# Loads, idle products and an order: the entry, the first pairs and the last down part of a two-FFN encoder block

## The chip, the cores and the metric

One core of one Trainium2 chip runs the whole block in one launch. The metric is the device time of that launch in microseconds, as the median of several runs. A profiled execution has a time of its own, and its span runs from the first instruction to the last.

## The reference

The kernel computes one layer on 512 tokens of width 1024, with 16 learned meta tokens set in front (528 columns in all), in float32:

```python
h = concat(meta, x)
f = swiglu(rmsnorm(h, g1), w_gate1, w_up1, w_down1)      # 1024 -> 2816 -> 1024
h = h + 0.5 * rmsnorm(f, post1)
h = h + rmsnorm(mixer(rmsnorm(h, mix_pre)), mix_post)    # two attentions, gated
f = swiglu(rmsnorm(h, g2), w_gate2, w_up2, w_down2)
h = h + 0.5 * rmsnorm(f, post2)
return h[16:]
```

with `swiglu(h) = (silu(h @ w_gate) * (h @ w_up)) @ w_down`. The two feed-forward blocks and their borders are what the change touches; the mixer between them stays as it is.

## The kernel before, in words

**Precision.** A float32 operand is split into a rounded high part (a cast on ScalarE, line 190) and a remainder (a subtraction on VectorE, line 195). Each product is three TensorE products of such parts, hi.hi, hi.lo and lo.hi (`mm3`, lines 165 to 169). Weights arrive as float32 through SyncE's DMA queue (line 157) and are split on arrival, so every weight tile costs a load, a cast and a subtraction.

**Order.** The program text is put in order by a scheduler that simulates the engines; instructions written inside `high_priority` go ahead of others that are ready, and `after(x)` puts an instruction behind `x` on `x`'s engine. On each engine, and in SyncE's queue, the order is then fixed and the engine works strictly in it.

**Buffers.** PSUM has eight tiles of 128 x 512, by tags: `z` (4), `b` (2), `y` (2). Scratch tiles of 128 x 528 are `T` (7 buffers, lines 108 and 64). Summed inputs and other split tiles share tag `u` (8 buffers).

**Entry** (`entry`, lines 292 to 333). The 528 columns go in two halves of 272 and 256. For the first half, eight input tiles are loaded, squared on ScalarE, and each square is summed over its partitions by one-column float32 products on TensorE (line 309). Mean, power -0.5 (on GpSimd, line 244) and a spread over the partitions (line 251) give the factor by which VectorE scales the inputs (line 325) before they are split. The loads of the second half (line 332) are issued after the first weight halves; its squares stand behind the splits of the first half, and its sums and chain come after them.

**Feed-forward block** (`ffn`, line 540). There are 22 tiles of 128 hidden units, in three phases of 6, 8 and 8; after each phase `down` adds the phase's share of the output. The tiles 0 and 1 (`first_two`, line 557) are multiplied half by half, four PSUM outputs side by side (`products`, line 572). Tiles 2 and 3 are `plain` (line 600). The other 18 go as nine pairs (`pair`, line 468): a two-by-two block product with seven products for gate and seven for up instead of eight, each of four k steps, in the order of `PAIR_ORDER` (line 30). Of these, `11`, `12` and `d` take the inputs as they are; `a`, `b`, `c` and `22` take sums of input tiles that `moving` (line 446) makes once per block, after the plain tiles: for each of four j, four half-width operations and two splits, with results named `mab` and `mcd`. On the weight side each pair needs the sums `ws` (lines 498 and 500).

**Down of the first block** (`down_cols`, line 639). In the last phase five column tiles are computed and handed to `post` one half at a time (lines 668 to 675); `post` (line 336) adds the earlier share from PSUM (line 344), squares, scales, multiplies with h, squares again, and adds three of these to running sums (line 357). The remaining three column tiles follow by halves in `emit`.

Of the kernel before, what the change touches and what calls it, by code (L numbers as in the profile page):

```python
# [9 lines left out]
F32 = mybir.dt.float32  # L10
F32R = mybir.dt.float32r
AF = mybir.ActivationFunctionType
# [5 lines left out]
P = 128  # L18
# [10 lines left out]
PHASES = ((0, 6), (6, 8), (14, 8))  # L29
PAIR_ORDER = "g11 g12 ga gb gc u11 u12 gd g22 ua ub uc u22 ud"  # L30
# [36 lines left out]
CHAIN_PRIO = 300  # L67
MLA_SCALE = float((64 + 32) ** -0.5)
# [13 lines left out]
class Block:  # L82
# [115 lines left out]
    def consts(self, cvec, ident, tri, ms):  # L198
        nc = self.nc

        def load(name, src, w):
            t = self.cp.tile([P, w], F32, name=name)
            (nc.scalar if name == "cv" else nc.sync).dma_start(t, src)
            return t
        self.cv = load("cv", cvec, V_END)
        pre = nc.scalar.preload_act_table_set("silu_and_others")
# [8 lines left out]
        def late(mixer):  # L215
            if not mixer:
                self.ident = load("ident", ident, P)
                return
# [73 lines left out]
    def entry(self, xT):  # L292
        nc = self.nc
        self.h = [self.S(f"h{k}") for k in range(KT)]
        self.hh = []
        for hf, half in enumerate(H528):
            w, ns = half.w, len(half.slices)
            sl = slice(half.c0, half.c0 + w)
            pn = self.y("nsum")
            nc.vector.memset(pn[:, 288:288 + ns], 0.0)  # L300
            for k in range(KT):
                if hf == 0:
                    nc.sync.dma_start(self.h[k][:, sl], xT[k, :, sl])
                q = self.T("sq")
                with self.after(self.first[k][0] if hf else None):
                    nc.scalar.activation(q[:, :w], self.h[k][:, sl], AF.Square)
                for s, (c, n) in enumerate(half.slices):
                    c -= half.c0
                    nc.tensor.matmul(pn[:n, 288 + s:289 + s], q[:, c:c + n], self.ones[:, 0:1], start=False,
                                     stop=k == KT - 1, skip_group_check=True)  # L310
            if hf == 0:
                self.late(False)
                yield
            with self.tc.high_priority(ENTRY_PRIO):
# [5 lines left out]
                self.spread(pn, r, half)  # L320
# [8 lines left out]
            if hf == 0:  # L329
                c = slice(w, L)  # L330
                for k in range(KT):
                    nc.sync.dma_start(self.h[k][:, c], xT[k, :, c])
# [113 lines left out]
    def moving(self, W):  # L446
# [4 lines left out]
        self.mv = {n: [] for n in ("11", "12", "a", "b", "c", "22", "d")}  # L451
# [1062 lines left out]
```

## Time and profile before

| | |
|---|---|
| median of 3 runs | 1246.59 us (1243.51 to 1247.79) |
| the profiled execution | 1245.64 us, span 1243.8 us |
| TensorE busy | 1196.5 us, 96% of the span |
| VectorE, ScalarE, GpSimd busy | 828.2, 636.3, 114.8 us |
| mean granted TensorE clock | 0.982 |
| chain that ended last | TensorE 77%, VectorE 10%, DMA 5%, ScalarE 3% |

A row of a timeline gives start, duration, engine, line of the code, operation, written tile, read tiles and shapes; xN says that N instructions were merged into it, and the brackets give the idle time of that engine just before it with what ended it. In a row of windows each engine has its busy time and, in parentheses, the number of its instructions; after the engines stand the granted TensorE clock (PEclk, 1.00 is full), the busy share of the DMA engines and their GB/s. PE is TensorE, PEld its weight loads, DVE VectorE, ACT ScalarE, POOL GpSimd, SP SyncE; SPq is SyncE's queue. Matmuls are pipelined, so neighbouring rows overlap.

### The profile page before, as it was taken

To read this page: it belongs to the slowest core of one execution; us is meant where nothing else is said; L and a number is where in the kernel's file an instruction comes from. 1 tells how busy PE (TensorE), PEld (TensorE's weight loads), DVE (VectorE), ACT (ScalarE), POOL (GpSimd) and SP (SyncE) were. 2 spreads that over 40 slices of the span, in tenths; PEclk is the share of its full clock that TensorE was granted. 3 is DMA by queue.
4 is the path that set the end of the run, shared out by engine and by line. 5 is a ranking of instruction groups with operands and counts; after the bars stand their busy time and mean duration, and the time that the engine had idled before them with its cause. 6 is when DMAs were issued, how large, how long until landed. Compare 5 with 4: busy or idle time off the path is not lost.

```text
span 1243.8 us, 20731 instructions
## 1 busy us (share of the span) xinstructions
PE 1196.5 (96%) x7950; PEld 1080.0 (87%) x7950; DVE 828.2 (67%) x1631; ACT 636.3 (51%) x1368; POOL 114.8 (9%) x189
## 2 busy tenths in 40 slices
PE   7999999999998999999999999999998999999997
PEld 7999999999998887878876777768887899889987
DVE  4493687468857854646666767489766588458855
ACT  4353465235545454656667657566354456325542
POOL 0000000000000001110010243270000000000004
PEclk9889999999998999999999999999899999999999
DMA  7123234322432341222223134353143224413351
GB/s 228 52 61 93 86 103 124 115 67 87 155 110 84 112 139 43 78 85 85 99 97 93 64 114 154 107 194 119 35 153 119 76 95 125 122 59 103 119 170 68
DMA packets 46594, 130.29 MB, mean 105 GB/s; under 512 B 5368, under 2 KB 8824, under 8 KB 46496
## 3 DMA queue, kind: packets, MB, share of 16 engines
q1 hardware_dynamic: 46352, 128.95, 32.3%
q8 instruction: 62, 1.02, 0.3%
q14 instruction: 36, 0.29, 0.1%
q10 hardware_dynamic: 144, 0.04, 0.0%
HBM read 114.99 MB, written 12.58 MB: 103 GB/s over the span
## 4 chain that ended last, share of the span: by engine, by line
PE 77%; DVE 10%; DMA 5%; ACT 3%; issue 3%; POOL 1%; SPq 1%; DVEq 0%; ACTq 0%; POOLq 0%
PE pu L167 4%; PE pu L169 4%; PE pg L167 4%; PE pu L168 4%; PE pg L168 3%; PE pg L169 3%; PE down L719 3%; PE down L718 3%; PE down L717 3%; DVE wp L195 2%; PE start L168 2%; PE start L169 2%; PE start L167 2%; PE gt L167 2%; PE gt L169 2%
## 5 line engine op out<-in xcount | busy, mean ns | idle before, releaser
L190 ACT CAST wp<-ws 128x512 fp32r<-128x512 f32 x144 | 87.3, 621 | 84.5 <-DVE ws L500 55.3
L195 DVE TENSOR_TENSOR wp<-ws,wp 128x512 fp32r<-128x512 f32 x144 | 96.8, 686 | 23.0 <-ACT wp L190 22.6
L195 DVE TENSOR_TENSOR wdl<-wdr,wdh 128x1024 fp32r<-128x1024 f32 (+1 forms) x42 | 49.1, 1170 | 48.6 <-ACT wdh L190 24.2
L190 ACT CAST wdh<-wdr 128x1024 fp32r<-128x1024 f32 (+1 forms) x42 | 42.4, 1009 | 58.1 <-PE pu L169 21.7
L167 PE MATMUL down<-g,wdh 128*128 128x272 f32 (+1 forms) x208 | 60.8, 296 | 4.1 <-DVE f L344 3.7
L167 PE MATMUL pu<-un,wp 128*128 128x264 f32 (+1 forms) x216 | 61.2, 284 | 0.0
L168 PE MATMUL pu<-un,wp 128*128 128x264 f32 (+1 forms) x216 | 60.7, 281 | 0.0
L168 PE MATMUL pg<-un,wp 128*128 128x264 f32 (+1 forms) x216 | 60.6, 282 | 0.0
L168 PE MATMUL down<-g,wdh 128*128 128x272 f32 (+1 forms) x208 | 60.6, 294 | 0.0
L169 PE MATMUL pu<-un,wp 128*128 128x264 f32 (+1 forms) x216 | 60.4, 282 | 0.1
L167 PE MATMUL pg<-un,wp 128*128 128x264 f32 (+1 forms) x216 | 60.5, 282 | 0.0
L169 PE MATMUL pg<-un,wp 128*128 128x264 f32 (+1 forms) x216 | 60.3, 282 | 0.0
L169 PE MATMUL down<-g,wdl 128*128 128x272 f32 (+1 forms) x208 | 60.2, 293 | 0.0
L718 PE MATMUL down<-wdl,g 128*128 128x512 f32 x144 | 56.8, 394 | 0.0
L719 PE MATMUL down<-wdh,g 128*128 128x512 f32 x144 | 56.0, 394 | 0.0
L717 PE MATMUL down<-wdh,g 128*128 128x512 f32 x144 | 54.0, 394 | 0.0
L190 ACT CAST wp<-wpr 128x512 fp32r<-128x512 f32 x54 | 32.1, 621 | 33.4 <-DMA wpr<-g2p 16.5
L167 PE MATMUL pg<-mcd,wp 128*128 128x264 f32 (+1 forms) x144 | 42.3, 294 | 3.1 <-ACT kept L490 3.0
L167 PEld LDWEIGHTS down<-g,wdh 128*128 128x128 f32 x208 | 40.8, 197 | 4.7 <-ACT p L362 3.9
L498 DVE TENSOR_TENSOR ws<-wpr 128x1024 f32<-128x1024 f32 x18 | 22.1, 1225 | 33.1 <-DMA wpr<-g1p 16.5
L169 PE MATMUL pu<-mab,wp 128*128 128x264 f32 (+1 forms) x144 | 41.1, 286 | 2.4 <-DVE wp L195 2.4
L168 PE MATMUL pg<-mab,wp 128*128 128x264 f32 (+1 forms) x144 | 41.2, 287 | 1.5 <-DVE mab L195 1.4
(465 smaller groups left out, 4363.1 us busy)
## 6 DMA issues: line engine op xcount, KB each, us to landing
wdr<-d SPq DMA_DIRECT2D x38, 512.0 KB, 3.5
wpx<-u1p SPq DMA_DIRECT2D x18, 512.0 KB
wpr<-g1p SPq DMA_DIRECT2D x18, 512.0 KB, 3.7
wpx<-u2p SPq DMA_DIRECT2D x18, 512.0 KB, 4.7
wpr<-g2p SPq DMA_DIRECT2D x18, 512.0 KB, 3.7
wgtr<-w_in SPq DMA_DIRECT2D x16, 512.0 KB, 3.6
wxr<-w_out SPq DMA_DIRECT2D x8, 512.0 KB, 3.7
gl<-gates SPq DMA_DIRECT2D x16, 256.0 KB, 4.5
```

The source lines that it names most:

```text
L167: mm(out, wh, xh, start=first, stop=False, skip_group_check=True)
L168: mm(out, wh, xl, start=False, stop=False, skip_group_check=True)
L169: return mm(out, wl, xh, start=False, stop=last, skip_group_check=True).ins
L190: self.cast = nc.scalar.copy(hi, src).ins
L195: return nc.vector.tensor_tensor(lo, src, hi.bitcast(F32), ALU.subtract).ins
L498: TT(*sums[m], ALU.add)
L717: mm(o, gt[:, 0, s], wh, start=fi == 0, stop=False, skip_group_check=True)
L718: mm(o, gt[:, 0, s], wl, start=False, stop=False, skip_group_check=True)
L719: mm(o, gt[:, 1, s], wh, start=False, stop=fi == nf - 1, skip_group_check=True)
```

## The change

It has five parts. In `entry`, both halves of all eight inputs are loaded ahead of the weights, squared, and the squares are added on VectorE into one tile `accx`, so that the partition sums need one product per slice of tokens; 16 products of a tile of ones with itself go on TensorE at the start, four behind the first half's sums and four behind its spread (`turn_over`, `WARM`). The identity matrix is loaded through ScalarE's queue. In `products`, two of the four PSUM outputs of a second half come from tag `b`, and the gate weights of tile 2 are asked for right after the second half's chain. `moving` runs in two parts, one ahead of each plain tile. The first pair of each block takes `FIRST_ORDER`, where `u11` and `u12` come third and fourth. And in the last phase of the first block's down, each column tile's two PSUM halves are added to one full-width scratch tile, on which `post` runs once.

```diff
@@ -27,6 +27,7 @@
 PHASES = ((0, 6), (6, 8), (14, 8))
+FIRST_ORDER = "g11 g12 u11 u12 ga gb gc gd g22 ua ub uc u22 ud"
 PAIR_ORDER = "g11 g12 ga gb gc u11 u12 gd g22 ua ub uc u22 ud"
@@ -65,6 +66,7 @@
 CHAIN_PRIO = 300
+WARM = 16, 4, 4
 MLA_SCALE = float((64 + 32) ** -0.5)
@@ -200,9 +202,10 @@
             t = self.cp.tile([P, w], F32, name=name)
-            (nc.scalar if name == "cv" else nc.sync).dma_start(t, src)
+            (nc.sync if name == "ms" else nc.scalar).dma_start(t, src)
             return t
         self.cv = load("cv", cvec, V_END)
+        self.ident = load("ident", ident, P)
         pre = nc.scalar.preload_act_table_set("silu_and_others")
@@ -212,10 +215,7 @@
 
-        def late(mixer):
-            if not mixer:
-                self.ident = load("ident", ident, P)
-                return
+        def late():
             trif = self.T("trif")
@@ -293,31 +293,41 @@
         self.hh = []
+        acc = self.tp.tile([P, 528], F32, name="accx", tag="acc", bufs=3)
+        idle = self.b("idle")
+
+        def turn_over(n, behind=None):
+
+            with self.after(behind):
+                for _ in range(n):
+                    nc.tensor.matmul(idle[:, :P], self.ones, self.ones, start=True, stop=True)
+        turn_over(WARM[0])
+        for half in H528:
+            sl = slice(half.c0, half.c0 + half.w)
+            for k in range(KT):
+                nc.sync.dma_start(self.h[k][:, sl], xT[k, :, sl])
+                q = acc if k == 0 else self.T("sq")
+                nc.scalar.activation(q[:, sl], self.h[k][:, sl], AF.Square)
+                if k:
+                    nc.vector.tensor_tensor(acc[:, sl], acc[:, sl], q[:, sl], ALU.add)
+        yield
         for hf, half in enumerate(H528):
             w, ns = half.w, len(half.slices)
             sl = slice(half.c0, half.c0 + w)
-            pn = self.y("nsum")
-            nc.vector.memset(pn[:, 288:288 + ns], 0.0)
-            for k in range(KT):
+            with self.tc.high_priority(ENTRY_PRIO):
+                pn = self.y("nsum")
+                nc.vector.memset(pn[:, 288:288 + ns], 1.0)
+                x = self.sums(pn, 288, acc, half)
                 if hf == 0:
-                    nc.sync.dma_start(self.h[k][:, sl], xT[k, :, sl])
-                q = self.T("sq")
-                with self.after(self.first[k][0] if hf else None):
-                    nc.scalar.activation(q[:, :w], self.h[k][:, sl], AF.Square)
-                for s, (c, n) in enumerate(half.slices):
-                    c -= half.c0
-                    nc.tensor.matmul(pn[:n, 288 + s:289 + s], q[:, c:c + n], self.ones[:, 0:1], start=False,
-                                     stop=k == KT - 1, skip_group_check=True)
-            if hf == 0:
-                self.late(False)
-                yield
-            with self.tc.high_priority(ENTRY_PRIO):
+                    turn_over(WARM[1], x)
                 hh = self.cp.tile([P, 4], F32, name=f"hh{hf}")
                 self.mean(hh[:, :ns], pn[:, 288:288 + ns], ns, 1.0 / D)
...
                 r = self.tiny("r")
                 self.rsqrt(r[:, :ns], hh[:, :ns], ns)
-                self.spread(pn, r, half)
+                x = self.spread(pn, r, half)
+                if hf == 0:
+                    turn_over(WARM[2], x)
                 done = []
@@ -326,10 +336,6 @@
             self.first = done
-            if hf == 0:
-                c = slice(w, L)
-                for k in range(KT):
-                    nc.sync.dma_start(self.h[k][:, c], xT[k, :, c])
             yield half
@@ -443,13 +449,14 @@
 
-    def moving(self, W):
+    def moving(self, W, tiles):
 
         nc = self.nc
         H = W // 2
         STT = nc.vector.scalar_tensor_tensor
-        self.mv = {n: [] for n in ("11", "12", "a", "b", "c", "22", "d")}
-        for j in range(4):
+        if tiles[0] == 0:
+            self.mv = {n: [] for n in ("11", "12", "a", "b", "c", "22", "d")}
+        for j in tiles:
             t1, t2 = self.tn[j], self.tn[j + 4]
@@ -465,7 +472,7 @@
 
-    def pair(self, srcs, W, ga, gb):
+    def pair(self, srcs, W, ga, gb, order):
 
@@ -506,7 +513,7 @@
         out = {"11": Y, "b": Y, "c": Y, "22": Y, "12": X, "a": Z, "d": Z}
-        for step in PAIR_ORDER.split():
+        for step in order.split():
             m, n = "gu".index(step[0]), step[1:]
@@ -570,7 +577,7 @@
             def products(half):
-                zz = [self.z("start") for _ in range(4)]
+                zz = [(self.b if half.c0 and o < 2 else self.z)("start") for o in range(4)]
                 c = slice(half.c0, half.c0 + half.w)
@@ -590,6 +597,8 @@
             h1 = next(start)
+            with self.after(self.first[-1][0] if fresh else self.ready):
+                self.ahead = self.wload(gate[2], 1024, "wg")
             acts(h0, zz)
@@ -601,8 +610,11 @@
             for src, n in ((gate[f], "wg"), (up[f], "wu")):
-                with self.hold(f == 2 and not fresh):
-                    wh, wl = self.wload(src, 1024, n)
+                if f == 2 and n == "wg":
+                    wh, wl = self.ahead
+                else:
+                    with self.hold(f == 2 and not fresh):
+                        wh, wl = self.wload(src, 1024, n)
                 o = self.two("gu")
@@ -622,17 +634,17 @@
                 elif f < NPL:
+                    x = f - 2
+                    self.moving(W, (2 * x, 2 * x + 1))
                     plain(f)
                     if f == TURN_AT and not fresh:
                         self.turn()
                     f += 1
-                    if f == NPL:
-                        self.moving(W)
                 else:
                     new_g(f)
                     new_g(f + 1)
                     x = (f - NPL) // 2
-                    self.pair([p[x] for p in pairs], W, g[f], g[f + 1])
+                    self.pair([p[x] for p in pairs], W, g[f], g[f + 1], PAIR_ORDER if x else FIRST_ORDER)
                     f += 2
@@ -665,6 +677,7 @@
                         acc(o, w, half, fi, f0, n)
+                f = self.T("f") if final else None
                 for half, o in outs:
@@ -672,7 +685,9 @@
                     else:
-                        self.post(m, half, o, *tail)
+                        nc.vector.tensor_tensor(f[:, half.c0:half.c0 + half.w], o, fg, ALU.add)
+                if final:
+                    self.post(m, Half(0, L, None), f, tail[0], False, tail[2])
         kept = {}
@@ -828,7 +843,7 @@
 
-        self.late(True)
+        self.late()
         next(start)
         ws = [self.wload(a["w_in"][W_G + j], 1024, "wgt", self.spare(j) if j < 2 else None) for j in range(4)]
         for hf in range(2):
```

## Rows read from the trace of the kernel before

**Rows 1.** The page, part 1: TensorE's busy time, share and instructions.

```profile
PE 1196.5 (96%) x7950; PEld 1080.0 (87%) x7950; DVE 828.2 (67%) x1631; ACT 636.3 (51%) x1368; POOL 114.8 (9%) x189
```

**Rows 2.** Timeline of TensorE in the entry.

```profile
3.58 8.73 PE L309 MATMUL nsum<-ones,sq 128*16 128x1 f32 x48 [3.58 <-ACT sq L306]
...
16.96 1.27 PE L167 MATMUL start<-un,wfh 128*128 128x272 f32 x4 [1.04 <-ACT un L190]
...
31.93 2.51 PE L309 MATMUL nsum<-ones,sq 128*128 128x1 f32 x22
35.47 1.22 PE L251 MATMUL nsum<-ident,r 128*128 128x128 f32 x4 [1.03 <-POOL r L244]
37.70 1.22 PE L167 MATMUL start<-un,wfh 128*128 128x256 f32 x4 [1.01 <-ACT un L190]
...
50.79 0.28 PE L167 MATMUL gu<-un,wgh 128*128 128x272 f32 x1
```

**Rows 3.** Windows: start:end, length, busy time of each engine, PEclk, DMA, GB/s.

```profile
3.00:9.00 6.00, 5.42 (x31) 5.27 (x31) 0.17 (x1) 3.18 (x8) 0.00 (x0) 1.00 0.88 239
16.90:20.50 3.60, 3.54 (x16) 3.54 (x17) 3.56 (x9) 3.60 (x11) 0.00 (x0) 1.00 0.43 118
37.70:41.20 3.50, 3.50 (x16) 3.50 (x17) 3.50 (x10) 1.96 (x5) 0.00 (x0) 0.50 0.02 5
85.40:92.40 7.00, 6.76 (x29) 6.14 (x30) 5.68 (x11) 4.50 (x9) 0.00 (x0) 0.52 0.41 136
93.00:100.00 7.00, 7.00 (x59) 7.00 (x59) 1.30 (x2) 2.55 (x5) 0.00 (x0) 1.00 0.38 103
389.40:392.70 3.30, 3.30 (x17) 3.30 (x17) 2.85 (x8) 1.58 (x4) 0.00 (x0) 0.51 0.01 2
933.00:942.00 9.00, 5.14 (x38) 4.32 (x36) 8.35 (x17) 4.65 (x10) 0.00 (x0) 1.00 0.23 65
```

**Rows 4.** Timeline of TensorE in the first block's first pair.

```profile
83.38 0.39 PE L169 MATMUL pu<-mab,wp 128*128 128x264 f32 x1 [0.90 <-DVE wp L195]
...
85.34 0.55 PE L167 MATMUL pg<-mab,wp 128*128 128x264 f32 x2 [0.83 <-ACT mab L190]
```

**Rows 5.** Timelines of VectorE and TensorE at the last down part's end.

```profile
388.29 1.09 DVE L357 TENSOR_TENSOR acc<-acc,p 128x256 f32<-128x256 f32 x3
...
388.52 0.36 PE L167 MATMUL down<-g,wdh 128*128 128x272 f32 x1 [3.70 <-DVE f L344]
```

**Rows 6.** Timeline of ScalarE in the entry.

```profile
3.10 0.83 ACT L306 ACTIVATE sq<-h 128x272 f32<-128x272 f32 x2 [0.66 <-DMA h<-xT]
...
6.59 1.23 ACT L306 ACTIVATE sq<-h 128x272 f32<-128x272 f32 x3 [0.71 <-DMA h<-xT]
...
9.62 2.68 ACT L190 CAST wfh<-wfr 128x512 fp32r<-128x512 f32 x4 [1.80 <-DMA wfr<-g]
```

**Rows 7.** Timeline of VectorE in the entry.

```profile
12.95 0.15 DVE L241 TENSOR_SCALAR hh<-nsum 128x3 f32<-128x3 f32 x1
...
25.06 1.00 DVE L195 TENSOR_TENSOR un<-h,un 128x272 fp32r<-128x272 f32 x2
```

**Rows 8.** Timeline of SyncE's queue: the first half's inputs.

```profile
0.72 3.71 SPq L303 DMA_DIRECT2D h<-xT  x8
```

**Rows 9.** The instructions on tile mx: ns min/median/max, first and last start, forms.

```profile
L195 DVE TENSOR_TENSOR mab<-mx,mab x8: 679/690/698, 74.7 to 937.6; 128x528 fp32r<-128x528 f32 x4, 128x512 fp32r<-128x512 f32 x4
...
L456 DVE TENSOR_TENSOR mx<-h x4: 420/424/425, 69.8 to 81.6; 128x264 f32<-128x264 f32 x4
```

**Rows 10.** Timeline of VectorE around the plain tiles of both blocks.

```profile
50.38 0.42 DVE L551 TENSOR_TENSOR silu<-start,silu 128x256 f32<-128x256 f32 x1 [7.35 <-ACT silu L550]
...
903.58 0.43 DVE L551 TENSOR_TENSOR silu<-start,silu 128x256 f32<-128x256 f32 x1 [5.80 <-ACT silu L550]
...
912.78 1.23 DVE L498 TENSOR_TENSOR ws<-wpr 128x1024 f32<-128x1024 f32 x1 [4.60 <-DMA wpr<-g2p]
```

**Rows 11.** Timeline of TensorE at the second block's second half.

```profile
886.49 0.73 PE L167 MATMUL start<-un,wfh 128*128 128x256 f32 x4 [0.90 <-ACT un L285]
```

## The prediction

> **What bounds the kernel now.** I read the page's busy shares first: TensorE is busy for 1196.5 of 1243.8 us [rows 1], so the time is TensorE's work plus the 47 us in which it stands still plus what the lower clock costs. Only those two can give anything back, since the change removes no product of the two feed-forward blocks. Then I read TensorE's timeline where the change acts, and windows of the same stretches.
>
> The entry comes first. From 3.58 to 12.31 us TensorE does one-column sums, the first product runs at 16.96, the last product of the first half ends about 31.9, the sums of the second half follow, and the second half's first product waits until 37.70. The gate products of tile 2, the third gate tile, begin at 50.79 [rows 2]. Two products of 3 parts, 8 k and 4 outputs are 96 matmuls, and at full clock one takes 7.00/59 = 0.119 us, so a half is 11.4 us. Here the halves take 15.0 and 13.1: in 3.6 and 3.5 us at their starts only 16 matmuls run, where 30 fit [rows 3]. That is the lower of the two levels, 1.2 GHz; the granted clock shows it as 0.50 in the second stretch and not in the first (1.00), so there I go by the counts.
>
> The second place is the first pair of the first block. TensorE waits 0.90 us for a weight remainder and 0.83 us for a cast of a summed input tile [rows 4], then runs 7.0 us at the lower level, 29 matmuls where 59 fit [rows 3]. The third is the same pair in the second block: in 933 to 942 TensorE is busy 5.14 of 9.00 us and VectorE 8.35 [rows 3]. The fourth is the end of the first block's last down part, a wait of 3.70 us for a PSUM evacuation on VectorE [rows 5], with 3.3 us at the lower level behind it [rows 3].
>
> **The change, part by part.**
>
> *Entry, first half.* Removed: 48 sum records of the first half, which keep TensorE until 12.31, 4.5 us after the last square ended at 7.82 [rows 2, 6]. Added: seven adds on VectorE (two ops of 272 columns took 1.00 us [rows 7]; in 3 to 9 us VectorE is busy 0.17 of 6.00 [rows 3]), of which one lies behind the last square, and six sum records at 8.73/48 = 0.18 us. The sums can end at 7.82 + 0.5 + 1.1 = 9.4, the mean runs then and not at 12.95 [rows 7], and by this the first product could start at 16.96 - 3.6 = 13.4. But 8 inputs of 128 KB go on SP's queue ahead of the four first weight halves. SP issues 8 in 3.71 us [rows 8], 16 in some 8, which the transfers cover: at 239 GB/s [rows 3] 1.05 MB more takes 4.4 us. So the first cast of a weight half moves from 9.62 to about 14.0, and four casts in a row take 2.68 us [rows 6], the last remainder a good 0.7 more: all four outputs are fed from 17.4. The second weight halves stand behind the same bytes as before and do not move. By 17.4 about 12 of the 96 matmuls are done; 84 x 0.119 = 10.0, and the sums and spread of the second half, now eight records in between, cost 1.0: the half ends at 28.4. VectorE must by then have given all eight input remainders. Before, it did this half's work in 15.96 to 26.06 [rows 7]; now four weight remainders more (4 x 0.69) and one of 1024 columns fewer (1.2) make 11.7 us from about 13.4, so 25.1. That is enough for TensorE's last k at 27, with 2 us to spare; with that cover gone the half ends as late as VectorE.
>
> *Entry, second half.* Squares, sums and scaling are done under the first half's products, so the wait from 31.9 to 37.7 goes. What is late next is PSUM: two of the four outputs are now in other buffers and start at once, the other two wait for silu and product of the first half, some 0.4 us beyond six matmuls. Then 11.4 us: end at 28.4 + 0.4 + 11.4 = 40.2, against 50.79. **Gain 10.5.** Bounds: the first product stays at 16.96 and the half keeps its 15.0, then 31.9 + 0.4 + 11.4 = 43.7, gain 7.0; or it starts at 13.4 and nothing holds it, then 37.6, gain 13.1. I stand between, because the weights' 14.0 is a transfer rate and not a choice of the order.
>
> *Idle products.* Sixteen of 128 columns are 32 records; the nearest row has four records in 1.22 us at the lower level [rows 2], so 16 take between 4.9 us (full) and 9.8 us, from 1.0 us on. At worst they hold the sums from 8.3 to 10.8, which the weights' 14.0 covers. The eight behind them are 16 records of 0.15 to 0.31 us in TensorE's own waits, except the last four, ahead of the first product, whose cover is the same. Their worth is the clock: up to 1.7 us (16 matmuls in 3.6 us instead of 1.9). Row against rule: before the first product TensorE had 8.73 us without a gap, and still 16.9 to 20.5 ran at the lower level [rows 2, 3]. The Trainium skill (TensorE: Matmul & The Clock Gate, What's actually happening) says that the default state is throttled and that recent busy-ness releases it. Taken as the profile's busy time, that would have the clock up before the first product already, and the idle products would be worth nothing, a sum of 19.0; this trace disagrees for one-column sums.
>
> *Queues.* The identity goes from SP to ScalarE's queue: one issue of some 0.4 us ahead of the table load, hidden by the 0.66 us that ScalarE waits for the first input [rows 6]. The squares of the second half (8 x 0.42) come ahead of the weight casts on ScalarE, where it waited for the weights and now waits longer. The mask table stays on SP. Zero each.
>
> *Summed inputs early (both blocks).* Four tiles, each four half ops of 0.42 and two remainders of 0.69 on VectorE [rows 9]: 3.07 x 4 = 12.3 us, which before fell into the first pair and now stand ahead of the two plain tiles, 6.15 each. What hides them: VectorE idles 7.35 us before the second half's silu in the first block, 5.80 and 4.60 us around the plain tiles of the second [rows 10]. With that cover gone each would delay a plain tile's weights by up to 6.15. In the first block the stalls are worth 0.90 + 0.83 + (59 - 29) x 0.119 = 5.3; the up factors that need no summed tile now come third and fourth and give VectorE 24 matmuls (2.9 us) more. I take **4.5** of it, bounds 0 and 5.3. In the second block 9.00 - 5.14 = 3.9; I take **3.4**, bounds 0 and 3.9. Next late is the weight remainder of each product, one in 1.46 us of TensorE.
>
> *Second block, second half's first products* in other PSUM buffers: they wait 0.90 us for an input cast, not for PSUM [rows 11]. Zero; bounds -1.6 (transposes and up tile that filled in there lose these buffers) and +0.9.
>
> *Last down part at full width.* Per column tile eight ops of half width become four: three halves take 1.09 us, so 8 x 0.36 = 2.9 [rows 5], against 4 x 0.66 = 2.6 (0.69 a lone one). Five tiles: 1.5 us of VectorE ahead of the late evacuation; if that takes as much off the 3.70 and half of the clock's 1.3 (17 matmuls where 28 fit [rows 3]), **2.3**. Bounds: +5.0 if wait and clock both go, -0.3 if an evacuation finds a full op ahead of it instead of a half one.
>
> **Sum**: 10.5 + 4.5 + 3.4 + 2.3 = 20.7, on the profiled execution's 1245.64: 1224.9. That run lies 0.95 under the median of 1246.59; I say **1225**.
>
> **Rivals.**
> - *Weights first.* ScalarE and VectorE cannot give weight halves and inputs together and the first half ends at 31.9 as before; only the gap goes. Entry 7.0, the rest as above: 1228.4. For: VectorE is full there. Against: 2 us to spare.
> - *Lower level again.* TensorE is nearly still between the idle products and the weights (8 to 14 us), the clock falls back, and the first stretch is as slow as before: 1.7 less, 1226.6. For: after the gap at 32 to 37 the granted clock was 0.50 [rows 3].
> - *No relief in the pairs.* The first wait there is for a weight remainder [rows 4]; if VectorE is as late without the summed tiles, 7.9 are missing: 1232.8. Against: 12.3 us less of its work in that stretch.
> - *Slower: summed tiles in front of plain weights.* VectorE works in order, and a 6.15 us block ahead of the remainder that TensorE needs next shows in full. Four blocks are 24.6, and the lower level behind each costs 1.6: 31.0 against a gain of 20.7, so 1255.9. It decides once two thirds of the blocks show on TensorE. Against: rows 10 hold idle time for nearly all.
> - *Nothing happens*: the order on the engines stays as it was, 1245.6.
>
> **How the numbers follow.** Chances: forecast 0.50, weights first 0.17, lower level 0.13, no relief 0.12, slower 0.05, nothing 0.03. About 0.3% (3.7 us) is what a measurement of this kernel can tell from no change. All cases but the last two are faster by more: 0.92 less 0.04 for smaller terms missing together, so faster 0.88, same 0.06, slower 0.06. The forecast's own range is 1219 to 1231. The low end 1216 has the entry at 13.1 and the stalls gone whole with the clock's part; the high end 1238 takes in no relief together with the entry at its bound, and leaves out the last two cases and the tails.
>
> **What would show it.** Right: the third gate tile's first product near 40 us with no gap between the halves; no TensorE wait over 0.5 us in the first pair of either block; granted clock 1.00 through the first pair; the wait at the last down part under 2.5 us. Wrong: a first product later than 17, TensorE waits for remainders in the plain tiles (a new place), or the 12.3 us of summed tiles still beside the pair's products. If the third gate tile comes after 44, the entry's sum is wrong.

## The result, and the profile after

The changed kernel takes 1214.55 us (median of 4 runs, 1213.73 to 1217.79); the kernel before, run beside it, 1245.05 (1241.04 to 1247.79). The ratio is 0.9762, 95% interval 0.9728 to 0.9797: faster by 30.5 us. The forecast was 1225 and a gain of 20.7, and the low end of its range, 1216, lies above the median. The profiled execution took 1213.73 us, its span is 1211.6, 32.2 less than before.

The page's part 1, TensorE, beside [rows 1]: 17.0 us less busy and 15.2 less idle.

```profile
PE 1179.5 (97%) x7928; PEld 1067.2 (88%) x7928; DVE 833.1 (69%) x1628; ACT 634.8 (52%) x1353; POOL 114.4 (9%) x189
```

The timeline of TensorE in the entry, beside [rows 2].

```profile
1.13 6.28 PE L303 MATMUL idle<-ones 128*128 128x128 f32 x32 [1.13 <-DVE ones L214]
8.75 0.74 PE L234 MATMUL nsum<-ones,accx 128*16 128x1 f32 x6 [1.34 <-DVE accx L312]
...
14.35 0.39 PE L169 MATMUL start<-un,wfh 128*128 128x272 f32 x1 [0.46 <-ACT un L192]
14.58 0.51 PE L234 MATMUL nsum<-ones,accx 128*128 128x1 f32 x4
...
26.33 0.28 PE L170 MATMUL start<-un,wfh 128*128 128x256 f32 x1
...
39.96 0.28 PE L169 MATMUL gu<-un,wgh 128*128 128x272 f32 x1
```

Six records of sums stand where 48 stood, and the second half's sums run between the first half's first and second product. The halves now overlap: two products of 256 columns run at 22.3 us (merged into a row that begins with 272), the others from 26.33, while those of 272 go on until 30.4. The third gate tile begins at 39.96, where the kernel before has 50.79.

Windows of the changed kernel: the first products; the first pair of block 1; that of block 2, as far behind the end of its block's plain tiles as the last of [rows 3]; the end of block 1's last down part.

```profile
14.30:17.90 3.60, 3.55 (x25) 3.28 (x26) 3.60 (x9) 3.60 (x9) 0.83 (x1) 1.00 0.82 303
72.40:79.40 7.00, 7.00 (x60) 7.00 (x59) 3.24 (x5) 3.27 (x7) 0.00 (x0) 1.00 0.63 206
907.30:916.30 9.00, 8.97 (x71) 8.38 (x71) 7.50 (x12) 5.81 (x11) 0.00 (x0) 1.00 0.59 193
376.00:382.00 6.00, 5.27 (x31) 5.04 (x30) 4.93 (x18) 2.66 (x5) 1.94 (x9) 0.72 0.26 87
```

Where [rows 3] have 29 matmuls in 7 us of the first pair, there are 60, and in block 2's 9 us 71 where there were 38. TensorE has no wait in the first pair of either block, and none for an evacuation in the last down part. At 376 to 382 the lower level still shows, 0.72 on average.

To see where 32 us went, the span is cut at TensorE's own marks into eight stretches. Each row of the table is one profiled execution. **A**: start to the first pair. **B**: from there to the end of block 1's first down part. **C**: to the start of its last one. **D**: the last down part. **E**: the mixer, to block 2's first product. **F**: to the end of its plain tiles, 2 and 3 (two expectations call this point the end of tile 2). **G**: from there to the end of its first down part; in block 2 the first pair begins before the last plain products end. **H**: the rest. The kernels e1 to e11 are those of the experiments; the profiled execution of e5 ran disturbed throughout (2277.55 us) and is left out, and the same kernel was profiled again as e11.

| kernel | A | B | C | D | E | F | G | H |
|---|---|---|---|---|---|---|---|---|
| before | 74.0 | 61.5 | 205.1 | 68.3 | 459.0 | 59.4 | 57.0 | 259.5 |
| after | 63.2 | 55.7 | 203.9 | 62.0 | 461.6 | 55.3 | 52.3 | 257.6 |
| e1, PSUM tag undone | 63.1 | 55.7 | 203.9 | 63.2 | 457.1 | 56.5 | 51.2 | 258.2 |
| e2, down part by halves | 63.5 | 55.7 | 203.9 | 67.9 | 456.0 | 59.0 | 51.0 | 257.9 |
| e3, no idle products | 64.6 | 55.7 | 203.9 | 63.0 | 458.7 | 59.8 | 50.6 | 258.9 |
| e4, summed tiles late | 63.4 | 59.2 | 203.9 | 63.0 | 458.3 | 56.5 | 57.2 | 258.4 |
| e6, before + full width | 75.4 | 60.5 | 203.9 | 62.0 | 461.8 | 57.0 | 57.0 | 257.9 |
| e7, before + PSUM tag | 74.3 | 61.7 | 204.1 | 69.1 | 459.4 | 56.6 | 56.7 | 258.4 |
| e8, spread late | 62.9 | 55.7 | 203.9 | 63.4 | 460.1 | 59.0 | 52.1 | 258.0 |
| e9, idle at the borders | 63.3 | 55.7 | 203.9 | 64.8 | 459.7 | 58.1 | 51.0 | 257.9 |
| e10, weights first | 65.1 | 55.7 | 203.9 | 62.0 | 458.2 | 54.1 | 52.2 | 257.9 |
| e11, old pair order | 63.2 | 55.7 | 203.9 | 62.0 | 462.1 | 56.8 | 51.7 | 258.8 |

Before to after: A 10.8, B 5.8, C 1.2, D 6.3, E -2.6, F 4.1, G 4.7, H 1.9. The forecast had 10.5, 4.5, 0, 2.3, 0, 0, 3.4, 0. D and F hold 8.1 of the 11.5 that it missed.

### The profile page after: what moved, and what is told of

It reads as the page before. It is cut to its first block, busy times and chain, and to the rows that moved or that the text cites. A ratio compares the mean times of both kernels' runs of the same rounds, so it can differ in the third digit from the quotient of the medians.

```text
span 1211.6 us, 20678 instructions
## 1 busy us (share of the span) xinstructions
PE 1179.5 (97%) x7928; PEld 1067.2 (88%) x7928; DVE 833.1 (69%) x1628; ACT 634.8 (52%) x1353; POOL 114.4 (9%) x189
## 4 chain that ended last, share of the span: by engine, by line
PE 86%; DVE 6%; ACT 3%; issue 2%; DMA 2%; POOL 1%; SPq 0%; DVEq 0%; ACTq 0%; POOLq 0%
PE pg L169 5%; PE pu L171 5%; PE pg L171 5%; PE pu L170 5%; PE pu L169 5%; PE pg L170 5%; PE down L732 3%; PE down L734 3%; PE down L733 3%; PE down L169 2%; PE down L171 2%; PE down L170 2%; PE gt L169 2%; PE gt L171 2%; PE gt L170 2%
## 5 line engine op out<-in xcount | busy, mean ns | idle before, releaser
L169 PE MATMUL pg<-un,wp 128*128 128x264 f32 (+1 forms) x216 | 60.5, 282 | 0.0
L169 PE MATMUL down<-g,wdh 128*128 128x272 f32 (+1 forms) x208 | 59.4, 290 | 0.4 <-ACT wdh L192 0.4
L170 PE MATMUL down<-g,wdh 128*128 128x272 f32 (+1 forms) x208 | 59.0, 287 | 0.0
L733 PE MATMUL down<-wdl,g 128*128 128x512 f32 x144 | 56.8, 394 | 0.0
L169 PE MATMUL pg<-mcd,wp 128*128 128x264 f32 (+1 forms) x144 | 41.0, 285 | 1.7 <-ACT kept L497 1.7
L171 PE MATMUL pu<-mab,wp 128*128 128x264 f32 (+1 forms) x144 | 40.9, 284 | 0.0
L171 PE MATMUL pg<-mcd,wp 128*128 128x264 f32 (+1 forms) x144 | 40.9, 284 | 0.0
L170 PE MATMUL pg<-mcd,wp 128*128 128x264 f32 (+1 forms) x144 | 40.8, 283 | 0.0
L170 PE MATMUL pu<-mab,wp 128*128 128x264 f32 (+1 forms) x144 | 40.8, 283 | 0.0
```

What stands on the lines that cost most here:

```text
L169: mm(out, wh, xh, start=first, stop=False, skip_group_check=True)
L170: mm(out, wh, xl, start=False, stop=False, skip_group_check=True)
L171: return mm(out, wl, xh, start=False, stop=last, skip_group_check=True).ins
L733: mm(o, gt[:, 0, s], wl, start=False, stop=False, skip_group_check=True)
```

## The experiments

**e1. The second half's first products back in one kind of PSUM buffer.**

```
-  zz = [(self.b if half.c0 and o < 2 else self.z)("start") for o in range(4)]
+  zz = [self.z("start") for o in range(4)]
```

> The changed kernel with all four PSUM outputs of a second half in tag z again. Theory A (the 4.1 us that the second block's start gained, forecast as 0, came from the PSUM tag: with free outputs the spread of the second half runs in the middle of the first half's products and no gap stands ahead of the second half): about 4 us slower there (span +4), with a TensorE gap of 1 us or more and the lower clock back at the second block's second half, and 0 to 1 us in the first block. Theory B (it came from the early gate weights of tile 2 or from the order around it): within 1 us of the changed kernel, no gap.

Measured: 1213.94 us (1211.00 to 1217.85), ratio 0.9749 (0.9721 to 0.9778). F 56.5, G 51.2, A 63.1: F and G together lose 0.1 us, A nothing, and TensorE has no wait between block 2's halves, so the buffers are not what pays in F. The prediction's zero for them holds, and the theory made after the result fell.

**e2. The last down part evacuated by halves again** (`post` for each half, as before).

> The changed kernel with the last down part evacuated by halves again. Theory A (full width alone bought the 6.3 us between the last pair's end and the mixer's first product): about 6 us slower there, with a TensorE wait of some 3.7 us for an evacuation and the lower clock behind it; and if the 2.6 us that the mixer lost also come from the order that full width leaves behind, the mixer is 2 to 3 us shorter, so 3 to 6 us slower in all. Theory B (the gain is from earlier weights or clock, not from full width): under 2 us there.

Measured: 1217.64 us (1216.63 to 1219.96), ratio 0.9783 (0.9760 to 0.9806). D is 67.9, nearly as in the kernel before (68.3), and TensorE waits 3.1 us for an evacuation. The whole loses less than D because E came out at 456.0.

**e6. The other way round: the kernel before with full width alone.**

```
+  f = self.T("f") if final else None
   for half, o in outs:
...
-      self.post(m, half, o, *tail)
+      nc.vector.tensor_tensor(f[:, half.c0:half.c0 + half.w], o, fg, ALU.add)
+  if final:
+      self.post(m, Half(0, L, None), f, tail[0], False, tail[2])
```

> The kernel before, with the last down part's evacuation at full width and nothing else of the change. Theory A (it is worth by itself what the run without it lost): the last down part of block 1 goes from 68.4 to 62.6 us, and the whole from 1245.05 to 1239.3, give or take 3 for the mixer's order. Theory B (most of that came from the rest of the change): 66 us as the prediction had it, 1242.7.

Measured: 1237.2 us (1234.86 to 1237.57), ratio 0.9941 (0.9923 to 0.9958). D falls to 62.0: the same 6.3 us with nothing else of the change. VectorE's timeline in the kernel before, at the fourth column tile and the first of the part's last three:

```profile
377.48 0.43 DVE L344 TENSOR_TENSOR f<-downb,fg 128x272 f32<-128x272 f32 x1
377.83 1.10 DVE L357 TENSOR_TENSOR acc<-acc,p 128x256 f32<-128x256 f32 x3
378.86 0.43 DVE L361 TENSOR_TENSOR p<-hx,fg 128x272 f32<-128x272 f32 x1
379.21 0.41 DVE L344 TENSOR_TENSOR f<-downy,fg 128x256 f32<-128x256 f32 x1
...
387.94 0.43 DVE L344 TENSOR_TENSOR f<-down,fg 128x272 f32<-128x272 f32 x1
```

And the same engine at the same tiles in e6:

```profile
372.71 0.43 DVE L676 TENSOR_TENSOR f<-downb,fg 128x272 f32<-128x272 f32 x1
373.07 0.41 DVE L676 TENSOR_TENSOR f<-downy,fg 128x256 f32<-128x256 f32 x1
373.40 0.70 DVE L357 TENSOR_TENSOR acc<-acc,p 128x528 f32<-128x528 f32 x1
...
381.98 0.43 DVE L344 TENSOR_TENSOR f<-down,fg 128x272 f32<-128x272 f32 x1
```

By halves, the second half's evacuation (L344) stands behind four operations on its neighbours, 1.73 us after the first one. At full width the two go back to back, 0.36 us apart, and only then the additions. In this part TensorE waits for an evacuation and for no addition. The evacuation at 387.94, which ends TensorE's wait of 3.70 us in [rows 5], comes at 381.98 in e6. Counted from the start of the part (340.64 and 339.80) that is 5.1 us earlier, more than the 1.5 us of VectorE's time that the prediction saw saved. The windows from that start to that evacuation, the kernel before first, then e6:

```profile
340.64:387.94 47.30, 44.17 (x360) 43.95 (x360) 32.39 (x65) 25.14 (x49) 0.10 (x1) 1.00 0.41 125
339.80:381.98 42.18, 42.18 (x346) 42.18 (x347) 29.24 (x47) 21.93 (x33) 0.10 (x1) 1.00 0.38 114
```

VectorE has 3.2 us less work ahead of the evacuation, in part because additions and a weight remainder of 1.22 us now stand behind it, and idles 2.0 us less: it waits that much less for weight casts of ScalarE, whose squares run at full width too (25.14 to 21.93 us busy). The new order, the time saved and ScalarE's share act together, and no run separates them. TensorE's wait is gone in e6, and the lower level behind it (the 3.3 us of [rows 3]) with it.

Not all of the 6.3 us is the evacuation's. TensorE runs the same products in the same order through D in eight of the kernels; D is 62.0 in four of them (after, e6, e10, e11) and 63.0 to 63.4 in the others (e1, e3, e4, e8), where a stretch at the lower level at its end lasts some 3 us longer. The window of 382 to 384 in e8, then in the changed kernel:

```profile
382.00:384.00 2.00, 2.00 (x10) 1.74 (x9) 0.86 (x3) 0.00 (x0) 0.00 (x0) 0.50 0.00 0
382.00:384.00 2.00, 2.00 (x17) 1.84 (x17) 0.93 (x4) 0.55 (x2) 0.00 (x0) 1.00 0.04 10
```

The kernel before (0.50 from 400 to 406) and e2 have the long stretch. Compared with the four kernels that have it too, full width is worth 4.5 to 5.3 us; the rest of the 6.3 goes with the clock.

**e3. No idle products** (`WARM = 0, 0, 0`).

> The changed kernel without any idle product. Theory A (they hold TensorE's clock up for the first products and cost nothing, since TensorE waits for inputs): the first 3 to 4 us of the first half at 1.2 GHz, tile 2's first gate product 1.5 to 2 us later than 39.96, and the same in the total. Theory B (the weights and VectorE set the pace of the first half): within 0.5 us, and the sums of the first half no later or up to 0.6 us earlier, since the eight records between sums and spread go.

Measured: 1217.7 us (1217.21 to 1221.23), ratio 0.9784 (0.9762 to 0.9806). The third gate tile begins at 41.4, 1.4 us later. TensorE's timeline in e3, and its window of the first products:

```profile
8.73 1.15 PE L234 MATMUL nsum<-ones,accx 128*16 128x1 f32 x6 [8.73 <-DVE accx L312]
...
12.07 1.76 PE L251 MATMUL nsum<-ident,r 16*128 16x16 f32 x6 [2.19 <-POOL r L244]
...
14.99 1.47 PE L169 MATMUL start<-un,wfh 128*128 128x272 f32 x4 [0.52 <-ACT un L192]
...
17.53 0.57 PE L170 MATMUL start<-un,wfh 128*128 128x272 f32 x1
17.91 0.43 PE L171 MATMUL start<-un,wfl 128*128 128x272 f32 x1
...
14.30:17.90 3.60, 2.89 (x10) 2.34 (x11) 3.60 (x10) 3.34 (x8) 1.08 (x1) 1.00 0.74 277
```

Ten matmuls where the changed kernel has 25, and 0.43 us for one where it has 0.29: the lower level, though the granted clock reads 1.00, as in the second row of [rows 3]. The Trainium skill (TensorE: Matmul & The Clock Gate, Seeing it yourself) warns that records of the clock have been seen to be unreliable; these two stretches bear that out, so durations decide. The first products are not the whole of the 1.4 us: without the idle products the six records of the sums take 1.15 us and not 0.74, the mean comes at 10.68 and not 9.62, and the first product at 14.99, 0.64 later. The rest of what e3 loses lies behind the entry, in F (59.8) above all.

**e10. The second half's inputs behind the first halves of the weights.**

```
       if k:
           nc.vector.tensor_tensor(acc[:, sl], acc[:, sl], q[:, sl], ALU.add)
+      if half.c0 == 0:
+          yield
-  yield
```

> The changed kernel, with the loads, squares and adds of the input's second half asked for behind the first halves of the four first weight tiles (ahead of their second halves, as in the kernel before), all else as it is. Theory A (what pays in the entry is that the sums no longer run on TensorE one by one; 1 MB of inputs ahead of the weights buys nothing): the first cast of a weight half comes at 9.7 us and not at 13.4, there is no gap between the halves, the third gate tile begins at 38 to 40 us, and the whole is 1212.5 to 1214.6. Theory B (the second half's inputs must be ahead, as in the prediction's rival of the weights first): a gap of 3 us or more between the halves, the third gate tile at 43 us or later, the whole at 1218.

Measured: 1213.96 us (1210.43 to 1215.31), ratio 0.9756 (0.9732 to 0.9779): not to be told from the changed kernel. The first cast of a weight half comes at 8.38 instead of 13.36, there is no gap of 3 us, but A is 1.9 longer and the third gate tile begins at 41.9. So theory B fell, and A holds for the whole but not for the entry; E (458.2) and F (54.1) give the 1.9 back. Windows of e10:

```profile
12.00:14.00 2.00, 2.00 (x9) 1.96 (x10) 1.44 (x4) 1.89 (x6) 0.00 (x0) 0.50 1.04 296
14.00:16.00 2.00, 2.00 (x11) 2.00 (x10) 2.00 (x7) 1.16 (x4) 0.00 (x0) 0.50 0.82 267
16.00:18.00 2.00, 2.00 (x11) 2.00 (x10) 2.00 (x7) 2.00 (x5) 0.00 (x0) 0.50 0.39 142
```

The last two of them, and a later one, in the changed kernel:

```profile
14.00:16.00 2.00, 1.65 (x12) 1.60 (x12) 2.00 (x6) 2.00 (x5) 0.00 (x0) 1.00 1.01 370
16.00:18.00 2.00, 2.00 (x17) 1.78 (x16) 2.00 (x6) 2.00 (x6) 0.83 (x1) 1.00 0.59 218
22.00:24.00 2.00, 1.47 (x12) 1.26 (x11) 2.00 (x6) 0.44 (x2) 0.00 (x0) 1.00 0.96 367
```

The order alone does not decide the level. Up to 38 us e9 and e11 have the same instructions in the same order on TensorE, VectorE and ScalarE as the changed kernel, and still run at the lower level until 16.5 and 16.8 us. The same three windows in e11:

```profile
14.00:16.00 2.00, 2.00 (x11) 2.00 (x11) 2.00 (x5) 2.00 (x6) 0.00 (x0) 0.50 1.02 363
16.00:18.00 2.00, 2.00 (x15) 2.00 (x15) 2.00 (x6) 2.00 (x6) 0.83 (x1) 0.80 0.46 166
22.00:24.00 2.00, 2.00 (x17) 1.83 (x16) 2.00 (x6) 0.45 (x2) 0.00 (x0) 1.00 0.96 367
```

The third gate tile begins there at 39.99 (e11) and 40.08 (e9), as in the changed kernel (39.96). What e11 loses it has made good by 24 us: in 22 to 24 TensorE of the changed kernel waits 0.53 us for a remainder from VectorE and e11 does not.

**e4. The summed input tiles late**, as before the change.

```
-  self.moving(W, (2 * x, 2 * x + 1))
   plain(f)
...
   f += 1
+  if f == NPL:
+      self.moving(W, (0, 1, 2, 3))
```

> The changed kernel with the summed input tiles made after both plain tiles, as before; the first pair keeps its new order. Theory A (the 5.9 and 4.6 us of the two first pairs come from taking 12.3 us of VectorE's work out of the pair): 8 to 10 us slower, TensorE waits for mab and weight remainders back in both first pairs. Theory B (putting the two up products third and fourth did most of it): under 3 us slower.

Measured: 1224.11 us (1221.49 to 1225.57), ratio 0.9827 (0.9804 to 0.9849): 9.6 slower than the changed kernel, theory A. B is 59.2 and G 57.2. TensorE's timeline in e4's first pair, and the window in its block 2:

```profile
72.05 0.39 PE L169 MATMUL pu<-mab,wp 128*128 128x264 f32 x1 [0.47 <-ACT wp L192]
73.86 0.39 PE L171 MATMUL pu<-mab,wp 128*128 128x264 f32 x1 [0.77 <-DVE wp L197]
76.35 0.39 PE L169 MATMUL pu<-mab,wp 128*128 128x264 f32 x1 [0.50 <-ACT wp L192]
...
909.80:918.80 9.00, 6.24 (x36) 5.61 (x36) 9.00 (x18) 5.05 (x9) 0.00 (x0) 0.85 0.26 76
```

TensorE's waits in up factors on summed inputs (here for the weights' casts and remainders) are back, VectorE is busy for all 9 us and TensorE does 36 matmuls there, half of what it does in the changed kernel.

**e5 and e11. The old order of factors in the first pair** (`FIRST_ORDER` set to the old text).

> The first pair of each block asks for its factors in the old order (two plain gate factors, three summed ones, then the plain up factors); all else as in the changed kernel. From the start of block 1's first pair to the end of its first down part the kernel before takes 61.6 us, the changed one 55.7, and with the summed tiles late 59.2. Theory A (the lead that the two plain up factors give VectorE is the other part of that gain): 58 us here, and some 1 to 2 us more in block 2 (52.3 there now), so 1217.5 to 1218.5. Theory B (the early summed tiles alone do it, the order is worth nothing once they are early): 55.7 and 52.3 within 0.5, 1214.6 within 1.

> The same kernel as in the run of the first pair's old order, for a profile: Theory A 58 us from the start of block 1's first pair to the end of its first down part, theory B 55.7 within 0.5. The times of that run (1215.9 beside 1214.55) speak for B or for something between; if between, the difference is to be seen as a wait of TensorE for a plain up factor's remainder.

Measured: 1215.9 us, ratio 0.9770 (0.9747 to 0.9793), and 1216.13 in the one run of e11. B is 55.7 and G 51.7, as in the changed kernel: theory B. With the tiles early the order is worth nothing. Whether it is worth something with them late is not shown: e4 (59.2) differs from the kernel before (61.5) in the order, but also in having no stretch at the lower level in B.

**e7. The kernel before with the other PSUM buffers alone** (e1's edit, the other way).

> The kernel before, with two of the second half's four first products in the other PSUM buffers and nothing else of the change. In its program the second block's spread stands 57 products behind that block's first product, where the kernel before has it 85 behind. Theory A (that place, not the buffers, sets the gap of the second block's start): first product to end of tile 2 goes from 59.3 to 55.5 there, block 1's entry stays (50.8 within 0.5), and the whole is 1241.3, give or take 3 for the mixer. Theory B (neither the place nor the buffers): 59.3, 1245.

Measured: 1241.76 us (1235.32 to 1244.63), ratio 0.9971 (0.9951 to 0.9990). F is 56.6: 2.8 of the 3.8 us expected, nearer to theory A, and TensorE's wait ahead of block 2's second half is gone. In block 1 the third gate tile begins at 39.0, but the first pair at 74.3 and not earlier: the tile's products only run among the second half's, which begin at 37.96 (before 37.70, [rows 2]); the wait ahead of both stays.

**e8. The spread held late in the changed kernel**, behind the last product of the seventh input tile.

```
-  marks.append(self.spread(pn, r2, half))
+  with self.after(self.lastp if half.c0 else None):
+      marks.append(self.spread(pn, r2, half))
...
   x = self.mm3(zz[o][:, :half.w], ws[o][0][:, s], ...)
+  if k < KT - 1:
+      self.lastp = x
```

> The changed kernel, with the second half's spread in block 2 held back behind the last product of the first half's seventh input tile, so that it stands 85 products behind the block's first one (58 in the changed kernel, 85 in the kernel before); nothing else. Theory A (the place of the spread sets the gap): first product to end of tile 2 goes from 55.3 to 58.5 to 59.3 us, the whole from 1214.6 to 1218.2. Theory B (it goes with something else in the order): 55.3 within 0.5, 1214.6.

Measured: 1217.89 us (1217.23 to 1219.91), ratio 0.9793 (0.9772 to 0.9813). F is 59.0, theory A. The timeline of the spread (nsum, L251) and what hangs on it, in the changed kernel:

```profile
857.93 0.60 PE L251 MATMUL nsum<-ident,r 128*128 128x128 f32 x4
...
858.57 0.38 ACT L399 COPY rbn<-nsum 128x256 f32<-128x256 f32 x1 [2.08 <-PE nsum L251]
```

and in e8:

```profile
862.31 0.60 PE L251 MATMUL nsum<-ident,r 128*128 128x128 f32 x4
...
862.95 0.37 ACT L401 COPY rbn<-nsum 128x256 f32<-128x256 f32 x1 [6.27 <-PE nsum L251]
...
866.59 0.74 PE L169 MATMUL start<-un,wfh 128*128 128x256 f32 x4 [1.40 <-ACT un L285]
867.82 0.39 PE L170 MATMUL start<-un,wfh 128*128 128x256 f32 x1 [0.26 <-DVE un L286]
```

ScalarE waits 6.27 us for the spread, and the second half's inputs are then late for TensorE by 1.40 and 0.26; in the changed kernel TensorE has no wait between the halves. The kernel before has the spread at 883.82, 15.9 us behind the block's first product (e8 16.3, the changed kernel 11.5), and a wait of 0.90 [rows 11].

The 85 of the expectations of e7 and e8 is a count of timeline rows, in which several products can be merged. By TensorE's records the spread stands behind 57 products of the first half in the changed kernel, 84 in e8 and all 96 in the kernel before. Over the twelve kernels: where it stands behind 84 to 96 (before, e2, e3, e4, e6, e8), TensorE waits 0.9 to 2.6 us for the second half's inputs; where it stands behind 56 to 60 (the other six), TensorE has no wait from the second half on.

Part of e8's 3.7 us is the clock. The first 10 us of block 2 in the changed kernel, e11 and e8:

```profile
846.38:856.38 10.00, 9.22 (x64) 9.13 (x65) 10.00 (x36) 3.27 (x9) 1.17 (x2) 0.83 0.00 0
846.92:856.92 10.00, 9.21 (x52) 9.12 (x52) 10.00 (x36) 3.10 (x8) 1.17 (x2) 0.66 0.00 0
846.06:856.06 10.00, 9.21 (x52) 9.13 (x52) 10.00 (x36) 3.10 (x8) 1.17 (x2) 0.66 0.00 0
```

e11 has the spread at 57 as the changed kernel has, and F is 56.8 there. So 1.5 of the 3.7 us come with the longer stretch at the lower level, and 2.2 with the spread's place.

**e9. Idle products at the block borders**, four of 128 columns behind the sums of each half.

> The changed kernel, with four idle products of 128 columns behind the one-column sums of each half at both borders of the blocks, into columns that the spread overwrites. In the changed kernel the granted clock is 0.57 to 0.58 in 378 to 382, 0.51 to 0.64 in 388 to 392 and 0.50 in 850 to 852, each time behind such sums and a short wait; compared with the usual spacing of the products these stretches cost 2.6, 2.4 and 2.2 us. Theory A (the clock falls because TensorE has nothing but one-column sums and waits there; four products hold it): no 2-us stretch under 0.9 there, and 2 to 5 us less, 1210 to 1212.5. Theory B (four are too few, or only push the spread back): the low stretches stay and the whole is 1215 to 1217.

Measured: 1216.45 us (1214.72 to 1218.17), ratio 0.9778 (0.9757 to 0.9799): theory B. Windows of e9 at the first border:

```profile
378.00:380.00 2.00, 1.17 (x5) 1.05 (x5) 1.58 (x6) 1.04 (x1) 0.85 (x1) 0.58 0.00 0
380.00:382.00 2.00, 1.95 (x10) 1.66 (x8) 1.23 (x7) 0.39 (x1) 0.00 (x0) 0.50 0.37 100
382.00:384.00 2.00, 1.62 (x7) 1.62 (x8) 2.00 (x8) 1.24 (x3) 1.06 (x7) 0.50 0.43 170
384.00:386.00 2.00, 2.00 (x13) 1.76 (x12) 1.37 (x5) 0.81 (x2) 0.00 (x0) 0.71 0.00 0
```

In the changed kernel the granted clock is 0.58, 0.57, 1.00 and 1.00 in these four. The first stretch at the lower level lasts until 385 and not 382, the second (388 to 392) is gone, the third lasts until 856 and not 853. Without idle products at the borders e1, e3, e4 and e8 have such a longer first stretch too, so it is not shown that these products made it longer; they did not prevent it. Of the versions tried, none is faster than the changed kernel by more than a measurement can tell.

## Why the prediction was right or wrong

**Entry: 10.5 forecast, 10.8 measured.** The working held at nearly each point: mean at 9.62 (forecast 9.4), first product at 14.35 (between 13.4 and 16.96), first weight cast at 13.36 (14.0), VectorE's last remainder of the half at 26.49 (25.1), third gate tile at 39.96 (40.2). What was not foreseen is that the halves overlap: the first half ends at 30.4 and not at 28.4, with products of the second among its own, and the sum comes out since TensorE waits only 0.53 us in between. The idle products are worth 1.4 (e3) within the "up to 1.7", but not by the clock of the first products alone, as the working had it: the sums and the mean come earlier by them too, and e11 keeps the lower level until 16.8 us and loses nothing. The rival *weights first* did not come: both halves are through at 39.96. e10 is 1.9 us longer in the entry, but also has the lower level until 18 us, and how much of the 1.9 is the place of the inputs is not shown; in the whole E and F hide it. *Lower level again* did come as a state: the granted clock fell to 0.50 between 10 and 13 us in the changed kernel and was back by the first products, in e9 and e11 it was not back until 16.5 and 16.8. The 1.7 us that this rival gave it were not lost there. That the changed kernel's profile has the full level from 14 us goes with that execution and not with the code.

**First pairs: 4.5 and 3.4 forecast, 5.8 and 4.7 measured.** Mechanism right: e4 gives 3.5 (B) and 4.9 (G) for the early tiles alone. My bounds, 5.3 and 3.9, taken from one window each, were too tight by 0.5 and 0.8. The step that the order gives VectorE "24 matmuls more" was worth nothing once the tiles are early (e11). *No relief* and the slower rival, *summed tiles in front of plain weights*, fell: A ends 23.2 us behind the third gate tile's first product, as before, and TensorE has no wait in the plain tiles of block 1: VectorE's idle time in [rows 10] was real cover.

**Last down part: 2.3 forecast, 6.3 measured.** This is the term that was mis-sized most, and above its bound of +5.0. The step that failed is "if that takes as much off the 3.70 and half of the clock's 1.3": I priced VectorE's time saved (1.5 us) and took that off the wait. The late evacuation came 5.1 us earlier in its part, by the new order on VectorE and shorter waits for ScalarE as well, which takes away the whole wait and the stretch at the lower level behind it (e2 and e6, from both sides). That is the case of the bound, and with the clock alike at the part's end it is worth 4.5 to 5.3 us; the last us or so of the 6.3 is luck, a shorter stretch at the lower level that other kernels with the same products do not have.

**Block 2's first products: zero forecast, 4.1 measured in F**, above the bound of +0.9. Here the step "they wait 0.90 us for an input cast, not for PSUM. Zero" failed. It was true of the buffers (e1), but I asked only what the edit does by itself. The program is put in order by a scheduler, and any edit moves other work: the second half's spread went from behind 96 products of the first half to behind 57, and the wait for the second half's inputs went with it. Holding it behind 84 costs 3.7 us in F (e8), 2.2 of them without the clock. That this is luck and not a part of the change shows in e2, e3 and e4, which have it behind 90 to 96 again with nothing of block 2's start edited. Its place does not tell all: e4 has it late and F 56.5, and kernels with it early have F from 54.1 to 58.1.

**Not forecast at all.** C gives 1.2 and H 1.9; both come with every edit of the table, e6 and e7 included, so they belong to the order of the kernel before or to its one profiled execution; which, no run shows. E, the mixer, which the change does not touch, took 456.0 to 462.1 in the twelve kernels, 2.6 more after than before. What sets it was not tried and stays open; it is of the size of the gains that it blurs.

In sum: entry and pairs made 18.4 of the 20.7 forecast and measured 21.3; the last down part gave 4.0 more than forecast, block 2's first products 4.1; C, E and H together 0.5.

## What to carry to other kernels

Where TensorE waits for an evacuation, look at what stands ahead of it in the evacuating engine's order: joining the halves, with two evacuations together ahead of the additions, was worth 4.5 to 5.3 us where counting the saved operations gave 2.3. In a kernel whose order comes from a scheduler, put a range of a few us on stretches that the edit does not touch, and measure each part both ways (taken out of the new kernel, put alone into the old one), stretch by stretch, since the total mixes them with the shuffle. Compare stretches only between executions with the same granted clock in them: here the same products took 1 to 1.5 us more or less by it. VectorE's additions moved into its real idle time cost TensorE nothing, as the idle rows said.

## What the runs showed of the hardware that was not expected

Idle products do not hold the clock by being there. In e9, with four behind each half's sums, the granted clock is 0.50 to 0.71 from 378 to 386 us, where it was 0.57 to 0.58 from 378 to 382 without them; another low stretch went. Nor does the same code get the same level each time: with 24 of them in the entry and the same instructions up to 38 us, the changed kernel is at the full level from 14 us, e9 and e11 only from 16.5 and 16.8; and with the same products in the last down part, the stretch at the lower level at its end is over at 382 us in the changed kernel and at 384 in e8. And the granted clock's record read 1.00 in e3 while products of 272 columns took 0.43 us, against 0.29 at the full level.
